# Splitting q and k on 128 partitions with DMA stacking, normalising dilated P on GpSimd, and merging differential P by one ratio, in a hybrid attention trunk

## The chip, the cores and the metric

The kernel runs on one core of a Trainium2 chip. The metric is the device time of one execution in microseconds. A core has five engines, each with its own queue of instructions that it works off in order: TensorE (PE, matrix products; its weight loads are listed as PEld), VectorE (DVE), ScalarE (ACT), GpSimd (POOL) and SyncE (SP), which here issues every DMA. Engines wait for each other by semaphores. TensorE writes to PSUM, the other engines mostly read and write SBUF, which has 128 partitions.

## The reference, cut to what matters

Two layers; each has two attention branches on the same RMS-normalised input of 512 tokens by 1024 features, all in float32.

```python
def dilated_mixture(q, k, v):            # branch A, 16 heads of 64
    outs = [dilated_pattern(q, k, v, w, d) for (w, d) in DILATED_PAIRS]   # softmax per pattern
    wts = d_all * jnp.exp(m_all - jnp.max(m_all, axis=0))                 # weighted by denominators
    return jnp.sum(wts[..., None] * o_all, axis=0) / jnp.sum(wts, axis=0)[..., None]

def one_block(args):                     # branch B, 8 heads with two q/k maps of 64, values of 128
    sc = jnp.einsum('mbqhd,mbkhd->mbhqk', qblk, ks) * (dh ** -0.5)        # causal mask follows
    p = jax.nn.softmax(sc, axis=-1)
    a = p[0] - lam * p[1]
    return jnp.einsum('bhqk,bkhe->bqhe', a, vf)
...
    qa = partial_rope(qa.reshape(b, s, A_HEADS, HEAD_DIM), cos, sin)      # also ka, qb, kb
    ob = rms_norm(ob, subln_w, SUBLN_EPS) * (1.0 - lam_init)
    merged = sigmoid(ga) * (ya @ w_proj_a) + sigmoid(gb) * (yb @ w_proj_b)
    return x + merged @ w_out
```

## The kernel before

Every product that has to be as exact as float32 is made of three float32r products: each operand is split into a part `hi` with fewer bits and the rest, `lo`, and `hi*hi + hi*lo + lo*hi` is summed in PSUM. A split is one ACT pass (the copy that rounds) and one DVE pass (the difference).

Weights come as 207 half chunks of 512 rows by 256 columns, 512 KB each, in the order of use. SP loads them into three buffers `raw` (L75); ACT writes `whi` (L84), DVE `wlo` (L85), and the buffer is free for the next load when DVE is through.

Projections come in two forms: `proj_T` (L164 to L166, tiles `pj`) gives two blocks of 128 features by 512 tokens, in 512-column matmuls; `proj_V` (L216 to L218, tiles `pv`) gives four blocks of 128 tokens by 256 columns. Attention heads are worked in units: a pair of heads in branch A (u = 0 to 7) and a head with its two maps in branch B (u = 0 to 7), 16 units per layer, written (layer, branch, u). While the projections of the next unit run on PE, the scores of the present unit and the values of the one before are spread between their steps (`run`, `mix`, L460 and L675). The order on each engine, and with it the semaphores, comes from a scheduler that simulates the program; it is not written out by hand, so a change of the passes also changes where other instructions stand.

The steps that matter here:

- **q and k** (`ev_qk`, L231): of the projection in PSUM, DVE makes a shuffled copy `sw` (L234) and the product with a cosine table (L236), POOL multiplies `sw` by the sine table (L237), DVE adds (L238). The result `rot` holds two heads (or maps), one on partitions 0 to 63 and one on 64 to 127. S needs q of a head as [hi; lo] stacked on 128 partitions, and k as [lo; hi] and [hi; lo] (tiles `qx`, and `kx` for either half). ACT and DVE write these on 64 partitions at a time: for q L243 to L246, for each half of k L252 to L255.
- **S** (`s_steps`): four blocks of queries per half; L300 and L305/L306 are the matmuls, L307 adds the bias and takes the row minimum (S is negated), L308 makes the exponential and its sum `den`.
- **Normalising** (`norm` in `a_pair`): DVE takes 1/den (L348) and multiplies P's four blocks of 128, 256, 384 and 512 columns by it (L351). In branch B `comb` (L397) scales both maps and adds them, the second with minus lambda (L404, L405).
- **P transposed and values**: L325 transposes P on PE, L326 and L327 split it, L359 and L415 are the products with V. V's own split is L270 and L271. In branch B each output row is then normalised by its root mean square: squares summed by ACT (L427), the inverse root on POOL (L132), four scalings on DVE (L432), and a transposition (`turn`).

Of the kernel before, what the change touches and what calls it, by code (L numbers as in the profile page):

```python
# [9 lines left out]
F32 = mybir.dt.float32  # L10
# [22 lines left out]
def trunk_kernel(ctx: ExitStack, tc: tile.TileContext, x, win, wpa, wpb, wout, norm_w, subln_w, final_w, lams,  # L33
# [24 lines left out]
    # ---------------------------------------------------------------- weights  # L58
    # Half chunks of 512 rows by 256 columns, in the order of use: loaded ahead, then split into
    # a part with float32r's 12 bits and the rest, which float32r holds exactly.  # L60
# [28 lines left out]
    # -------------------------------------------------------------- constants  # L89
# [13 lines left out]
    # P transposed; pt1 keeps a block of zeros  # L103
# [7 lines left out]
    # ------------------------------------------------------ residual and norm  # L111
    def h_block(layer, m, xt):
        """hi and lo parts of x * norm_w; 1/rms comes in after the projections"""
        h = b4(f"h{layer}_{m}")
        nc.scalar.activation(h[:, 0], xt, AF.Copy, scale=nw[:, layer, m:m + 1])  # L115
        nc.vector.scalar_tensor_tensor(h[:, 1], xt, nw[:, layer, m:m + 1], bits(h[:, 0]), OP.mult, OP.subtract)  # L116
        st_["hnew"][m] = h

    def sq_block(m, xt):
        """the running sum of squares, but for the last block's"""  # L120
# [13 lines left out]
    def rstd_cols():  # L134
        """per-token 1/rms as columns [token, token block]"""
# [23 lines left out]
    # ------------------------------------------------------------ projections  # L159
    def mm3(ps, hb, wi, kk, c0, first, last):  # L160
        """ps += w[:, c0:c0+128].T @ h over one block of 128 rows, in three passes"""
# [8 lines left out]
    def proj_T(rhs, evac, first=False):  # L170
        """Two output blocks, features on partitions. rhs(k) gives the moving block."""
# [27 lines left out]
    def proj_V(lhs, evac):  # L199
        """256 columns, tokens on partitions. lhs(k) gives the stationary block."""  # L200
# [29 lines left out]

    def ev_qk(key):  # L231
        def f(b, ps):
# [6 lines left out]
            lo, hi = slice(0, 64), slice(64, 128)  # L239
            if b == 0:  # L240
                qx = b4(f"qx{key}")
                # S' = -scale * q.k: the sign makes the row maximum a minimum
                nc.scalar.activation(qx[lo, 0], r[lo], AF.Copy, scale=-SCALE)  # L243
                nc.scalar.activation(qx[hi, 1], r[hi], AF.Copy, scale=-SCALE)
                nc.vector.scalar_tensor_tensor(qx[hi, 0], r[lo], -SCALE, bits(qx[lo, 0]), OP.mult, OP.subtract)
                nc.vector.scalar_tensor_tensor(qx[lo, 1], r[hi], -SCALE, bits(qx[hi, 1]), OP.mult, OP.subtract)  # L246
                st_["qk"][key] = [qx]
            else:
                # against a head's [hi; lo] of q: [lo; hi] of k, and [hi; lo] of k
                for half, (mine, other) in enumerate(((lo, hi), (hi, lo))):  # L250
                    kx = b4(f"kx{key}{half}")
                    nc.scalar.activation(kx[mine, 1], r[mine], AF.Copy)  # L252
                    nc.vector.tensor_tensor(kx[mine, 0], r[mine], bits(kx[mine, 1]), OP.subtract)
                    nc.scalar.activation(kx[other, 0], bits(kx[mine, 1]), AF.Copy)
                    nc.vector.tensor_copy(kx[other, 1], bits(kx[mine, 0]))  # L255
# [3 lines left out]
    def ev_v(key, br):  # L259
        def f(tb, ps):  # L260
# [4 lines left out]
            # per head: the columns' hi parts, then their lo parts  # L265
# [18 lines left out]
    # -------------------------------------------------------------- attention  # L284
    def s_steps(key, half, br, store):
# [6 lines left out]
        def s(i):  # L292
# [5 lines left out]
            if i == 0:  # L298
                # 256 columns hold both products, which float32r's full rate needs
# [33 lines left out]
    def pt_block(j, i, s):  # L333
        """P transposed: keys of block j, queries of block i"""
# [5 lines left out]
    def a_pair(layer, u):  # L340
        """two heads of the dilated mixture"""
# [4 lines left out]
        def norm(half):  # L346
            r = small.tile([P, 4], F32, tag="r", name=f"r{key}{half}")
            nc.vector.reciprocal(r, store["den", half])  # L348
            for i in range(4):
                p = store["p", half][i]  # L350
                nc.vector.tensor_scalar(p, p, r[:, i:i + 1], None, OP.mult)  # L351
# [39 lines left out]
    def b_head(layer, u):  # L391
        """one head of the differential attention"""
# [402 lines left out]
```

## Time and profile before

| | |
|---|---|
| median of 3 runs | 1399.28 us (1399.16, 1399.28, 1399.30) |
| span of the profiled execution | 1397.3 us |
| PE busy | 1380.0 us (99%) |
| DVE busy | 1047.4 us (75%) |
| ACT busy | 795.7 us (57%) |
| POOL busy | 152.5 us (11%) |
| DMA, mean over the span | 94 GB/s |

The span is that of the instructions in the profiled execution; the time of a run also holds what lies around it, some 2 us. An engine's busy time counts the time in which it executes, not that in which it waits. The profile names an instruction by engine, line and tile, and where an engine stood idle before it, the length of that and what released it. "s(0, 0, 3)10" is block 0 of half 1 of the unit (0, 0, 3).

### The profile page before, as it was taken

The page shows a single profiled execution, that of the slowest core. Times are in us where ns is not written, and L with a number is a line of the kernel's source. Part 1 is how long each engine was busy: PE and PEld are TensorE (multiplying, and loading weights), DVE is VectorE, ACT ScalarE, POOL GpSimd, SP SyncE. Part 2 cuts the span into 40 slices and gives each one's busy share as a digit, 9 for nine tenths or more (in the row PEclk, how much of TensorE's full clock was granted, in tenths as well). Part 3 has the DMA queues.
Part 4 walks back from the last instruction along what each step waited for, and adds up shares of the span by engine and source line. Part 5 has one row for each costly group of instructions (what it writes and reads, how often), then busy time and mean ns, then how long its engine had stood idle before and what let it go on. Part 6 is the DMA issues. An engine that isn't in the chain of part 4 may idle for free.

```text
span 1397.3 us, 20366 instructions
## 1 busy us (share of the span) xinstructions
PE 1380.0 (99%) x7592; PEld 1192.9 (85%) x7592; DVE 1047.4 (75%) x2188; ACT 795.7 (57%) x1530; POOL 152.5 (11%) x123
## 2 busy tenths in 40 slices
PE   7999999999999999999999999999999999999998
PEld 6888898989888888888888888988888988888898
DVE  6899989985678886445558989999865889763554
ACT  4666666665456666333445767666645666653333
POOL 3201000100101111110211000110000111111000
PEclk9999999999999999999999999999999999999999
DMA  6222212223331233332532212122233222333421
GB/s 215 97 61 76 76 61 86 66 76 106 113 98 62 73 109 121 106 106 91 188 99 82 70 61 91 61 76 76 83 114 106 76 76 76 98 113 120 152 90 62
DMA packets 41954, 131.66 MB, mean 94 GB/s; under 512 B 4864, under 2 KB 4992, under 8 KB 41856
## 3 DMA queue, kind: packets, MB, share of 16 engines
q1 hardware_dynamic: 41856, 130.38, 28.8%
q8 instruction: 59, 0.97, 0.3%
q14 instruction: 39, 0.32, 0.1%
HBM read 121.97 MB, written 8.39 MB: 93 GB/s over the span
## 4 chain that ended last, share of the span: by engine, by line
PE 86%; DVE 10%; issue 2%; ACT 1%; DMA 0%; POOL 0%; SPq 0%; POOLq 0%; DVEq 0%; ACTq 0%
PE pj L164 20%; PE pj L165 20%; PE pj L166 20%; PE pv L216 4%; PE pv L218 4%; PE pv L217 4%; DVE wlo L85 2%; DVE pt L327 1%; DMA x<-x_d 0%; DVE h L116 0%; PE xt L553 0%; PE ps_ss L140 0%; ACT whi L84 0%; ACT h L115 0%; POOL rf L570 0%
## 5 line engine op out<-in xcount | busy, mean ns | idle before, releaser
L164 PE MATMUL pj<-h,whi 128*128 128x512 f32 x1024 | 409.8, 402 | 6.3 <-DVE whi L610 6.0
L165 PE MATMUL pj<-h,whi 128*128 128x512 f32 x1024 | 404.8, 396 | 1.0 <-DVE h L116 0.9
L166 PE MATMUL pj<-h,wlo 128*128 128x512 f32 x1024 | 403.7, 396 | 0.1
L85 DVE TENSOR_TENSOR wlo<-raw,whi 128x1024 fp32r<-128x1024 f32 x207 | 273.0, 1320 | 85.4 <-ACT whi L84 84.6
L84 ACT ACTIVATE whi<-raw 128x1024 fp32r<-128x1024 f32 x207 | 218.3, 1055 | 148.9 <-PE pj L165 104.3
L164 PEld LDWEIGHTS pj<-h,whi 128*128 128x128 f32 x1024 | 193.4, 189 | 41.8 <-issue 6.0
L166 PEld LDWEIGHTS pj<-h,wlo 128*128 128x128 f32 x1024 | 193.0, 188 | 40.1 <-DVE wlo L85 0.5
L165 PEld LDWEIGHTS pj<-h,whi 128*128 128x128 f32 x1024 | 193.4, 189 | 35.8 <-DVE h L116 2.7
L216 PE MATMUL pv<-whi,h 128*128 128x256 f32 x512 | 146.7, 287 | 2.2 <-DVE v(0, 0, 0)_0_399 L271 1.6
L217 PE MATMUL pv<-wlo,h 128*128 128x256 f32 x512 | 144.9, 283 | 0.0
L218 PE MATMUL pv<-whi,h 128*128 128x256 f32 x512 | 144.8, 283 | 0.0
L216 PEld LDWEIGHTS pv<-whi,h 128*128 128x128 f32 x512 | 97.5, 190 | 4.5 <-DVE v(0, 0, 0)_0_399 L271 1.8
L217 PEld LDWEIGHTS pv<-wlo,h 128*128 128x128 f32 x512 | 97.6, 191 | 0.9
L218 PEld LDWEIGHTS pv<-whi,h 128*128 128x128 f32 x512 | 97.5, 191 | 0.0
L506 POOL TENSOR_TENSOR g<-g,pr 128x512 f32<-128x512 f32 x16 | 21.7, 1354 | 162.4 <-ACT g L505 162.4
L503 DVE TENSOR_TENSOR g<-pj,rb 128x512 f32<-128x512 f32 x32 | 21.8, 688 | 23.4 <-PE pj L166 23.3
L217 PE MATMUL pv<-wlo,mg 128*128 128x256 f32 x128 | 35.8, 283 | 0.0
L218 PE MATMUL pv<-whi,mg 128*128 128x256 f32 x128 | 35.7, 283 | 0.0
L216 PE MATMUL pv<-whi,mg 128*128 128x256 f32 x128 | 35.4, 283 | 0.0
L514 DVE TENSOR_TENSOR g<-pj,g 128x512 f32<-128x512 f32 x16 | 11.1, 692 | 30.5 <-PE pj L166 30.5
L126 POOL TENSOR_TENSOR sq<-sq,sq 128x512 f32<-128x512 f32 x12 | 19.2, 1598 | 85.8 <-ACT sq L122 85.5
L518 ACT ACTIVATE mg<-g 128x512 fp32r<-128x512 f32 x16 | 10.1, 631 | 29.5 <-DVE g L515 29.5
(4991 smaller groups left out, 2903.8 us busy)
## 6 DMA issues: line engine op xcount, KB each, us to landing
raw<-win_d SPq DMA_DIRECT2D x159, 512.0 KB, 3.5
raw<-wpa_d SPq DMA_DIRECT2D x16, 512.0 KB, 3.5
raw<-wpb_d SPq DMA_DIRECT2D x16, 512.0 KB, 3.5
raw<-wout_d SPq DMA_DIRECT2D x16, 512.0 KB, 3.5
pa_dram<-pa SPq DMA_DIRECT2D x16, 256.0 KB, 2.0
pr<-pa_dram SPq DMA_DIRECT2D x16, 256.0 KB, 3.9
xr<-x_d SPq DMA_DIRECT2D x8, 256.0 KB, 4.1
x_dram<-xr SPq DMA_DIRECT2D x8, 256.0 KB, 2.6
```

The costliest lines, as they stand in the source:

```text
L84: nc.scalar.activation(whi[j], raw[j], AF.Copy)
L85: nc.vector.tensor_tensor(wlo[j], raw.pop(j), bits(whi[j]), OP.subtract)
L126: nc.gpsimd.tensor_tensor(st_["acc"], st_["acc"], s, OP.add)
L164: nc.tensor.matmul(ps, w_h, hb[:, 0], start=first, stop=False)
L165: nc.tensor.matmul(ps, w_h, hb[:, 1], start=False, stop=False)
L166: nc.tensor.matmul(ps, w_l, hb[:, 0], start=False, stop=last)
L216: nc.tensor.matmul(ps, hh, whi[wi][:, k % 4], start=(k == 0), stop=False)
L217: nc.tensor.matmul(ps, hh, wlo[wi][:, k % 4], start=False, stop=False)
L218: nc.tensor.matmul(ps, hl, whi[wi][:, k % 4], start=False, stop=(k == 7))
L327: nc.vector.tensor_tensor(dst[:, 1], ps[:, :n], bits(dst[:, 0]), OP.subtract)
L503: nc.vector.tensor_tensor(g[:, b], ps, rb, OP.mult)
L506: nc.gpsimd.tensor_tensor(g[:, 0], g[:, 0], st_.pop(("pa", m)), OP.mult)
```

## The change

`ev_qk` makes the hi and the lo part of q, and of k, in one pass each on all 128 partitions, into a new tile `hl` (from the same pool of 27 buffers). SP then copies 64-partition pieces by DMA into `qx` (four moves of 128 KB) and `kx` (per half one move of 256 KB and two of 128 KB). In branch A the four multiplications of P by 1/den go from DVE to POOL. In branch B P is merged as p1 + q*p2 with q = -lambda*den1/den2, without the scaling of p1 by r = 1/den1, which is applied with the output: in the squares (as `scale`) and in one pass that multiplies the output by r times the inverse root.

```diff
+    def move(to, of):
+        nc.sync.dma_start(bits(to), bits(of))
 ...
-            lo, hi = slice(0, 64), slice(64, 128)
+            hl = b4(f"hl{key}{b}")
+            f_ = -SCALE if b == 0 else 1.0
+            nc.scalar.activation(hl[:, 1], r, AF.Copy, scale=f_)
+            nc.vector.scalar_tensor_tensor(hl[:, 0], r, f_, bits(hl[:, 1]), OP.mult, OP.subtract)
             if b == 0:
                 qx = b4(f"qx{key}")
-                nc.scalar.activation(qx[lo, 0], r[lo], AF.Copy, scale=-SCALE)
-                nc.scalar.activation(qx[hi, 1], r[hi], AF.Copy, scale=-SCALE)
-                nc.vector.scalar_tensor_tensor(qx[hi, 0], r[lo], -SCALE, bits(qx[lo, 0]), OP.mult, OP.subtract)
-                nc.vector.scalar_tensor_tensor(qx[lo, 1], r[hi], -SCALE, bits(qx[hi, 1]), OP.mult, OP.subtract)
+                for half in range(2):
+                    mine = slice(64 * half, 64 * half + 64)
+                    move(qx[0:64, half], hl[mine, 1])
+                    move(qx[64:128, half], hl[mine, 0])
                 st_["qk"][key] = [qx]
             else:
-                for half, (mine, other) in enumerate(((lo, hi), (hi, lo))):
+                for half in range(2):
                     kx = b4(f"kx{key}{half}")
-                    nc.scalar.activation(kx[mine, 1], r[mine], AF.Copy)
-                    nc.vector.tensor_tensor(kx[mine, 0], r[mine], bits(kx[mine, 1]), OP.subtract)
-                    nc.scalar.activation(kx[other, 0], bits(kx[mine, 1]), AF.Copy)
-                    nc.vector.tensor_copy(kx[other, 1], bits(kx[mine, 0]))
+                    mine = slice(64 * half, 64 * half + 64)
+                    move(kx[0:64], hl[mine])
+                    move(kx[64:128, 0], hl[mine, 1])
+                    move(kx[64:128, 1], hl[mine, 0])
 ...
-                nc.vector.tensor_scalar(p, p, r[:, i:i + 1], None, OP.mult)
+                nc.gpsimd.tensor_scalar(p, p, r[:, i:i + 1], None, OP.mult)
 ...
-            r = [small.tile([P, 4], F32, tag=f"rb{h}", name=f"rb{key}{h}") for h in range(2)]
-            for h in range(2):
-                nc.vector.reciprocal(r[h], store["den", h])
-            nc.vector.tensor_scalar(r[1], r[1], nlam[:, layer:layer + 1], None, OP.mult)
+            r = small.tile([P, 4], F32, tag="rb0", name=f"rb{key}")
+            q = small.tile([P, 4], F32, tag="rb1", name=f"rq{key}")
+            nc.vector.reciprocal(q, store["den", 1])
+            nc.vector.reciprocal(r, store["den", 0])
+            nc.vector.scalar_tensor_tensor(q, q, nlam[:, layer:layer + 1], store["den", 0], OP.mult, OP.mult)
+            store["r"] = r
             for i in range(4):
                 p, p2 = store["p", 0][i], store["p", 1][i]
-                nc.vector.tensor_scalar(p, p, r[0][:, i:i + 1], None, OP.mult)
-                nc.vector.scalar_tensor_tensor(p, p2, r[1][:, i:i + 1], p, OP.mult, OP.add)
+                nc.vector.scalar_tensor_tensor(p, p2, q[:, i:i + 1], p, OP.mult, OP.add)
 ...
+                r = store["r"][:, i:i + 1]
-                nc.scalar.activation(scr, o[:, n], AF.Square, accum_out=store["ss"][:, i:i + 1])
+                nc.scalar.activation(scr, o[:, n], AF.Square, scale=r, accum_out=store["ss"][:, i:i + 1])
 ...
-                for i in range(4):
-                    nc.vector.tensor_scalar(store["o"][:, i], store["o"][:, i], r[:, i:i + 1], None, OP.mult)
+                nc.vector.tensor_tensor(r, r, store["r"], OP.mult)
+                o = store["o"]
+                nc.vector.tensor_tensor(o, o, r.unsqueeze(2).to_broadcast([P, 4, P]), OP.mult)
```

The scheduler puts instructions in another order. On PE, at the first unit of layer 0, the kernel before has the end of the fourth block of V's projection (`pv_3`), six matmuls of the next q projection (`pj_0`), and then the first S:

```order
L216 MATMUL pv_3_457<-whi_334,h_7_172 128x256
L217 MATMUL pv_3_457<-wlo_335,h_7_172 128x256
L218 MATMUL pv_3_457<-whi_334,h_7_172 128x256
L164 MATMUL pj_0_515<-h_0_123,whi_368 128x512
L165 MATMUL pj_0_515<-h_0_123,whi_368 128x512
L166 MATMUL pj_0_515<-h_0_123,wlo_369 128x512
L164 MATMUL pj_0_515<-h_1_128,whi_368 128x512
L165 MATMUL pj_0_515<-h_1_128,whi_368 128x512
L166 MATMUL pj_0_515<-h_1_128,wlo_369 128x512
L300 MATMUL s(0, 0, 0)00_522<-kx(0, 0, 0)0_358,qx(0, 0, 0)_316 128x256
```

The changed kernel has there, on the same engine, at the end of the third block (`pv_2`):

```order
L216 MATMUL pv_2_433<-whi_337,h_7_172 128x256
L217 MATMUL pv_2_433<-wlo_338,h_7_172 128x256
L218 MATMUL pv_2_433<-whi_337,h_7_172 128x256
L307 MATMUL s(0, 0, 0)00_526<-kx(0, 0, 0)0_364,qx(0, 0, 0)_319 128x256
L312 MATMUL s(0, 0, 0)01_538<-kx(0, 0, 0)0_364,qx(0, 0, 0)_319 128x256
L313 MATMUL s(0, 0, 0)01_538<-kx(0, 0, 0)0_364,qx(0, 0, 0)_319 128x256
L216 MATMUL pv_3_461<-whi_279,h_0_123 128x256
```

S of the first two blocks of queries has moved ahead of the whole fourth block, 24 matmuls, and of the six of the q projection. It is the same in layer 1.

On SP, at units (0,0,6) and (0,0,7), the queue of the kernel before holds weight loads alone:

```order
L75 DMA raw_2224<-win_d 128x1024
L75 DMA raw_2264<-win_d 128x1024
L75 DMA raw_2351<-win_d 128x1024
L75 DMA raw_2415<-win_d 128x1024
L75 DMA raw_2498<-win_d 128x1024
L75 DMA raw_2550<-win_d 128x1024
```

In the changed kernel the moves of a unit stand between them (x2 is two alike in a row):

```order
L75 DMA raw_2292<-win_d 128x1024
L232 DMA qx(0, 0, 7)_2347<-hl(0, 0, 7)0_2344 64x512 x2
L75 DMA raw_2382<-win_d 128x1024
L232 DMA qx(0, 0, 7)_2347<-hl(0, 0, 7)0_2344 64x512 x2
L75 DMA raw_2447<-win_d 128x1024
L232 DMA kx(0, 0, 7)0_2422<-hl(0, 0, 7)1_2419 64x512
L232 DMA kx(0, 0, 7)0_2422<-hl(0, 0, 7)1_2419 64x1024
L232 DMA kx(0, 0, 7)0_2422<-hl(0, 0, 7)1_2419 64x512
L232 DMA kx(0, 0, 7)1_2426<-hl(0, 0, 7)1_2419 64x1024
L232 DMA kx(0, 0, 7)1_2426<-hl(0, 0, 7)1_2419 64x512 x2
L75 DMA raw_2530<-win_d 128x1024
```

Ten moves per unit now stand in the one queue with the weights.

## Rows read from the trace of the kernel before

**Rows 1.** The page's first part: busy time, share of the span and number of instructions of each engine.

```profile
PE 1380.0 (99%) x7592; PEld 1192.9 (85%) x7592; DVE 1047.4 (75%) x2188; ACT 795.7 (57%) x1530; POOL 152.5 (11%) x123
```

**Rows 2.** The waits of PE, the whole answer: who waited for whom, total us, times, longest us.

```profile
PE pj L164 <- DVE whi L610: 6.0, 1, 6.0
PE pv L216 <- DVE v(0, 0, 0)_0_399 L271: 1.6, 1, 1.6
PE pj L165 <- DVE h L116: 0.9, 1, 0.9
PE s(1, 0, 3)10_7983 L300 <- DVE mn(1, 0, 3)0_7812 L307: 0.7, 1, 0.7
PE s(0, 0, 3)10_1457 L300 <- DVE mn(0, 0, 3)0_1286 L307: 0.5, 1, 0.5
PE pv L216 <- DVE v(1, 0, 1)_0_7383 L271: 0.3, 1, 0.3
PE pv L216 <- DVE v(0, 0, 1)_0_857 L271: 0.3, 1, 0.3
PE pj L164 <- DVE v(1, 1, 3)_1_11531 L271: 0.2, 1, 0.2
PE pj L164 <- DVE v(0, 1, 3)_1_5005 L271: 0.2, 1, 0.2
```

**Rows 3.** Timeline of PE, 42 to 56 us: start, length (pipelined, so longer than the distance to the next), engine, line, output and inputs; in brackets idle time before it and its releaser.

```profile
42.99 0.28 PE L218 MATMUL pv<-whi,h 128*128 128x256 f32 x1
44.90 0.39 PE L216 MATMUL pv<-whi,h 128*128 128x256 f32 x1 [1.63 <-DVE v(0, 0, 0)_0_399 L271]
...
47.88 0.40 PE L164 MATMUL pj<-h,whi 128*128 128x512 f32 x1
...
49.27 0.28 PE L300 MATMUL s(0, 0, 0)00_522<-kx(0, 0, 0)0_358,qx(0, 0, 0)_316 128*128 128x256 f32 x1
...
53.29 0.39 PE L164 MATMUL pj<-h,whi 128*128 128x512 f32 x1
...
55.33 0.39 PE L165 MATMUL pj<-h,whi 128*128 128x512 f32 x1
```

**Rows 4.** Timeline of ACT and of DVE at the first unit of layer 0, columns as above.

```profile
40.34 0.63 ACT L243 ACTIVATE qx(0, 0, 0)_316<-rot(0, 0, 0)0_312 64x512 fp32r<-64x512 f32 x1 [2.46 <-DVE rot(0, 0, 0)0_312 L238]
...
41.23 0.69 DVE L245 SCALAR_TENSOR_TENSOR qx(0, 0, 0)_316<-rot(0, 0, 0)0_312,qx(0, 0, 0)_316 64x512 fp32r<-64x512 f32 x1
...
42.21 0.69 DVE L246 SCALAR_TENSOR_TENSOR qx(0, 0, 0)_316<-rot(0, 0, 0)0_312,qx(0, 0, 0)_316 64x512 fp32r<-64x512 f32 x1
...
44.37 0.48 DVE L271 SCALAR_TENSOR_TENSOR v(0, 0, 0)_0_399<-pv,rstd,v(0, 0, 0)_0_399 128x256 fp32r<-128x256 f32 x1
```

**Rows 5.** The page's part on DMA issues (count, KB each, median us from issue to landing), and two issues in a row from SP's timeline at the start.

```profile
raw<-win_d SPq DMA_DIRECT2D x159, 512.0 KB, 3.5
...
pa_dram<-pa SPq DMA_DIRECT2D x16, 256.0 KB, 2.0
...
1.65 0.42 SPq L596 DMA_DIRECT2D raw<-win_d  x1
2.12 0.43 SPq L595 DMA_DIRECT2D x<-x_d  x1
```

**Rows 6.** Timelines of DVE, ACT and PE at the first unit of layer 1.

```profile
723.80 1.68 DVE L238 TENSOR_TENSOR rot(1, 0, 0)0_6853<-rot(1, 0, 0)0_6853,sw(1, 0, 0)0_6851 128x512 f32<-128x512 f32 x1
...
725.51 0.63 ACT L243 ACTIVATE qx(1, 0, 0)_6857<-rot(1, 0, 0)0_6853 64x512 fp32r<-64x512 f32 x1 [1.52 <-DVE rot(1, 0, 0)0_6853 L238]
...
727.96 0.69 DVE L246 SCALAR_TENSOR_TENSOR qx(1, 0, 0)_6857<-rot(1, 0, 0)0_6853,qx(1, 0, 0)_6857 64x512 fp32r<-64x512 f32 x1
...
735.25 0.28 PE L300 MATMUL s(1, 0, 0)00_7048<-kx(1, 0, 0)0_6899,qx(1, 0, 0)_6857 128*128 128x256 f32 x1
```

**Rows 7.** Timelines of DVE, ACT and PE: k of unit (0,0,4) from its add to its first S, and the reciprocal and the first transpose of unit (0,0,3), half 0.

```profile
141.29 0.69 DVE L238 TENSOR_TENSOR rot(0, 0, 4)1_1414<-rot(0, 0, 4)1_1414,sw(0, 0, 4)1_1412 128x512 f32<-128x512 f32 x1
...
142.73 0.62 ACT L252 ACTIVATE kx(0, 0, 4)0_1418<-rot(0, 0, 4)1_1414 64x512 fp32r<-64x512 f32 x1
...
143.09 0.16 DVE L348 RECIPROCAL r(0, 0, 3)0_1400<-den(0, 0, 3)0_1287 128x4 f32<-128x4 f32 x1
...
146.68 0.42 DVE L255 CAST kx(0, 0, 4)0_1418<-kx(0, 0, 4)0_1418 64x512 fp32r<-64x512 f32 x1
...
152.69 0.28 PE L300 MATMUL s(0, 0, 4)00_1645<-kx(0, 0, 4)0_1418,qx(0, 0, 4)_1346 128*128 128x256 f32 x1
...
154.20 0.27 PE L325 MATMUL t((0, 0, 3), 0)0_1657<-ident,p(0, 0, 3)00_1304 128*128 128x128 f32 x1
```

**Rows 8.** The waits of SP's DMA queue, first row: total us, times, longest us.

```profile
SPq L75 <- DVE wlo L85: 719.2, 125, 13.8
```

**Rows 9.** Instructions of the lines L237 and L351: count, then shortest, median and longest ns, and start.

```profile
L237 POOL TENSOR_TENSOR sw(0, 0, 0)0_310<-sw(0, 0, 0)0_310,st x1: 1305/1305/1305, 36.1 to 36.1; 128x512 f32<-128x512 f32 x1
L237 POOL TENSOR_TENSOR sw(0, 0, 0)1_352<-sw(0, 0, 0)1_352,st x1: 2279/2279/2279, 37.3 to 37.3; 128x512 f32<-128x512 f32 x1
...
L351 DVE TENSOR_SCALAR p(0, 0, 0)00_523<-p(0, 0, 0)00_523,r(0, 0, 0)0_575 x1: 288/288/288, 59.9 to 59.9; 128x128 f32<-128x128 f32 x1
...
L351 DVE TENSOR_SCALAR p(0, 0, 0)03_570<-p(0, 0, 0)03_570,r(0, 0, 0)0_575 x1: 480/480/480, 60.7 to 60.7; 128x512 f32<-128x512 f32 x1
```

**Rows 10.** Busy time by stretches, from 9 to 13 us: length, then busy us and instructions of PE, PEld, DVE, ACT and POOL; granted clock, DMA's busy share, GB/s.

```profile
9.00:13.00 4.00, 4.00 (x18) 3.18 (x18) 2.98 (x5) 4.00 (x7) 0.67 (x1) 1.00 1.04 400
```

## The prediction

> **What bounds the kernel now.** I read the busy shares first: PE is busy 1380.0 of 1397.3 us, DVE 1047.4, ACT 795.7, POOL 152.5 [rows 1]. With an engine at 99%, work taken off the others is worth only the time for which PE waits for them, so the second view is the list of PE's waits, and it is the whole budget: 6.0 us and 0.9 us at the start (the first weights and the first h), 1.6 us before the fourth block of the first V projection, and six of 0.7 down to 0.2 us, 2.2 us together [rows 2]. The change touches neither the start nor the tail. It can win at most 1.6 + 2.2 = 3.8 us of waits, 0.27%; whatever it makes PE wait anew is lost in full. So the question is where PE is close behind its inputs, and this is at the first head of each layer.
>
> The granted clock is 1.00 throughout. PE's own pace: from 47.88 to 49.27 us six 512-column matmuls start in 1.39 us, 0.232 each; from 53.29 to 55.33, when DVE stands idle, nine start in 2.04 us, 0.227 each [rows 3]. I come back to that 2% as a rival.
>
> **The change part by part, q and k.** Before, a head's split costs ACT 6 and DVE 6 passes on 64 partitions, and S waits for the last of kx. Now ACT and DVE make one 128-partition pass each per block (4 in all) and SP issues ten SBUF-to-SBUF moves per head, four for qx and three for each kx, 1.5 MB. A pass on 128 partitions costs what one on 64 does (0.69 us for DVE's q pass on 64 [rows 4] and for its rope add on 128 [rows 7]), so 8 passes per head go. That frees time on engines which do not bound; what counts is when the first kx is there. Two moving parts: the issue on SP, 0.47 us from one to the next when they stand back to back [rows 5], and the flight. No row shows a transfer from SBUF to SBUF. The nearest are the 256 KB store of A's projection, 2.0 us from issue to landing, and the 512 KB weight load, 3.5 us [rows 5]; moves of 128 and 256 KB lie nearer the first. I bound the last landing by these two, and take 2.7.
>
> *First head of layer 0.* ACT begins q's hi at 40.34 and, in one pass, ends at 40.97. DVE's q pass starts at 41.23 and k's takes the place of the second q pass, at 42.21, and ends near 42.9 [rows 4]. SP issues q's moves from 41.0 on, k's first three at 42.95, 43.42 and 43.9. So kx for S0 lands between 45.9 and 47.4. Meanwhile the order on PE changes: S0 stands right behind block 2 of the V projection, where it stood behind block 3 and six more matmuls. PE is through block 2 at 43.27 (the last matmul starts at 42.99 and takes 0.28), and before, it then lost 1.63 us to the v evacuation, going on at 44.90 [rows 3]. That wait goes, as DVE comes to the evacuation (44.37 before [rows 4]) without the two kx passes ahead of it; but S0's wait stands in the same place and ends later. Net loss: 45.9 - 44.9 = 1.0 to 47.4 - 44.9 = 2.5; I take +1.7. The score reductions on DVE and the exponentials on ACT now stand ahead of the next weight split, which moves with S0; by an estimate from these passes' lengths it is still ready about 1 us before PE needs it, so it adds nothing.
>
> *First head of layer 1.* The same order on PE. S0 started at 735.25 [rows 6]; without block 3 (24 matmuls at 0.12 us, 2.88) and six at 0.232 (1.39) ahead of it, it is due at 730.98. ACT's q pass ends at 726.14 and DVE's k pass takes the place of the second q pass, ending near 728.65 [rows 6]. Three issues: 728.7, 729.2, 729.65; landing 731.65 to 733.15. Loss 0.7 to 2.2, I take +1.5. There was no wait here before to set against it.
>
> *The other 30 heads.* In the order, 17 to 22 us of PE work lie between the end of a k projection and its S0 for A heads (13.5 us for the second head of a layer), and more for B. In head (0,0,4) the k chain runs from DVE's add at 141.29, behind the product on POOL, to the last copy of the first kx, 146.68 + 0.42 = 147.1; S0 comes at 152.69 [rows 7]. Now: add ends 141.98, ACT's hi, behind what is queued there, again at 142.73 and until 143.4, lo until 144.1, three issues 1.4, flight 2.0 to 3.5: 147.5 to 149.0. That leaves 3.7 us. I cost these heads at nothing; the cover is those 3.7 us, and beyond it each us counts per head. Each DMA of SP's queue also waits for the one eight places earlier in the queue; in a burst of ten this reaches back to the head's own q moves, issued some 2 us or more earlier, so only kx's second half can feel it.
>
> SP's queue carries the weights as well. 320 issues at 0.33 to 0.47 us are about 130 us of SP's time, and moves that wait for DVE hold the next weight load behind them. But the loads now wait 719 us in 125 cases, up to 13.8 us, for a buffer to come free [rows 8], and a load is used several projections later: a delay of a few us is covered. Zero.
>
> **Normalising on GpSimd.** DVE loses per half four passes of 0.29 to 0.48 us, 1.5 together [rows 9], and POOL gets them. No row shows this pass on POOL. Bounds: 1.5 us if it goes at DVE's speed, 5.2 if each costs the 1.30 of POOL's 128x512 product, 9.0 if each costs the 2.28 that this product took beside DVE work [rows 9]. I take 4, nearer the undisturbed product. Its readers are the transposes: in head (0,0,3) the reciprocal comes at 143.09 and the first transpose at 154.20, 11 us later [rows 7]; over all halves of the new order the stretch from the last S matmul to the first transpose is at least 12 us of PE work, of which reduction, exponential and reciprocal take some 4. Hidden up to about 8 us. Behind it on POOL stands the next head's rope product, and behind that DVE's add, which blocks DVE's queue: this too is covered at 4 us. The two engines slow each other (DVE's add took 0.69 in head (0,0,4) and 1.68 beside POOL at the start of layer 1 [rows 6, 7]), at worst 1 us per collision on a chain that has 3.7. Zero, with the far bound kept for a rival.
>
> [...]
>
> **The merge in B.** Per head four TENSOR_SCALARs (the shapes of [rows 9], 1.5 us) and four of 0.28 become one pass over the output. PE has no wait on this chain in [rows 2]. Gain 0. Some 250 more semaphore waits on PE's queue run ahead of execution: 0.
>
> **The later waits.** The six of 2.2 us hang on DVE being late by less than 1 us (the reduction of S, v's evacuation) [rows 2]. DVE has 1.5 us less per half and eight passes less per head ahead of them. I count all 2.2 as won.
>
> **Sum.** +1.7 + 1.5 - 2.2 = +1.0 us. The profiled execution spans 1397.3; the median of 1399.28 has 2.0 us around the span, and the three runs lie within 0.01%, so the same 2.0 is added: 1397.3 + 1.0 + 2.0 = **1400.3**. Bounds by the two landings: 1.0 + 0.7 - 2.2 = -0.5 to 2.5 + 2.2 - 2.2 = +2.5, 1398.8 to 1401.8.
>
> **Rivals.**
> *Moves at half rate.* The moves go from 64 partitions to 64, and may use half of what a 128-partition load gets. The fastest stretch moved 400 GB/s [rows 10]; at 200, the 1 MB of q and of the first kx's bytes lasts 5.2 us from 41.0, and with the 1.4 to 2.0 us of a store's flight that is not bytes, it lands at 47.6 to 48.2: +3.0. In layer 1 a weight load lies between: 733.3 to 733.9, +2.6. Sum 3.0 + 2.6 - 2.2 = +3.4, 1402.7, just slower. For it: the shape; against it: the issue at 0.47 us per 128 KB is nearly as slow.
>
> [...]
>
> *POOL or SP blocks head by head* (ends slower). Place: the rope product behind the normalising on POOL, DVE's add behind it. Decides when a half costs POOL over about 8 us, or a move's flight exceeds 7. Price: 1 us beyond the cover in each of some 26 heads, +26: 1426. For it: 2.28 us in [rows 9]; against: the same product takes 1.30 where DVE is not in its way [rows 9].
>
> *The later waits don't go,* since DVE's order there is new too: +1.7 + 1.5 + 0 = +3.2, 1402.5.
>
> *PE's pace.* If the 2% between the two stretches of [rows 3] came from what the engines beside it do, and half of DVE's relief gave it back in the two A parts of some 215 us each: 430 x 1% = -4.3, sum -3.3, 1396.0, faster. For it: DVE is idle in one stretch and not in the other; against it: nothing in [rows 2] names an engine for it.
>
> **How the numbers follow.** Forecast 0.50 (1400.3; within 0.2%). Half rate 0.20 (three quarters slower, one quarter within). Head by head 0.10 (slower). Later waits stay 0.10 (half slower). Pace 0.10 (faster). Measurement of this kernel can tell about 0.2%, 2.8 us, from no change. Faster 0.10; slower 0.15 + 0.10 + 0.05 = 0.30, and with the upper tail of the forecast 0.33; same 0.57. The range 1396.0 to 1404.5 takes in all but the head-by-head case and the ends.
>
> **What would show it.** PE's list of waits: a wait of S(0,0,0)0 on SPq of 2.6 to 4.1 us in place of 1.6 on L271, one of 0.7 to 2.2 for S(1,0,0)0, and no entries of L307 or L271. The moves' landing in the DMA part: 2.0 to 3.5. The normalising rows on POOL: under 8 us a half. I am wrong if PE waits for other heads' kx or for transposes, or if its 512-column pace changes.

## The result: 0.72% slower, and the profile after

The changed kernel takes 1409.46 us (median of 4 runs, 1407.22 to 1411.30) against 1399.22 for the kernel before; the ratio is 1.0072, 95% interval 1.0057 to 1.0086. The forecast was 1400.3 with a range of 1396.0 to 1404.5. The profiled execution spans 1409.5 us, 12.2 more than the one of before.

First the busy shares of the changed kernel, which answer to [rows 1]:

```profile
PE 1384.4 (98%) x7592; PEld 1197.9 (85%) x7592; DVE 914.5 (65%) x1836; ACT 718.2 (51%) x1402; POOL 317.9 (23%) x251
```

DVE lost 133 us of work and ACT 78, and none of it came out at the end. PE's waits in the changed kernel say why; they answer to [rows 2] (total us, times, longest us):

```profile
PE pj L164 <- DVE whi L621: 5.9, 1, 5.9
PE s(1, 0, 0)00_7068 L307 <- DMA kx(1, 0, 0)0_6921<-hl(1, 0, 0)1_6918: 5.6, 1, 5.6
PE s(0, 0, 0)00_526 L307 <- DMA kx(0, 0, 0)0_364<-hl(0, 0, 0)1_361: 5.1, 1, 5.1
PE pj L165 <- DVE h L116: 1.1, 1, 1.1
PE s(1, 0, 1)00_7225 L307 <- DMA kx(1, 0, 1)1_7204<-hl(1, 0, 1)1_7197: 0.9, 1, 0.9
```

The 1.6 us on v's evacuation and the six small waits are gone. In their place S of the first unit waits for its moves, 5.1 us in layer 0 and 5.6 in layer 1, and the second unit of layer 1 waits 0.9.

That is not all. PE's timeline around the wait in layer 0 (answers to [rows 3]):

```profile
43.19 0.28 PE L217 MATMUL pv<-wlo,h 128*128 128x256 f32 x1
43.31 0.28 PE L218 MATMUL pv<-whi,h 128*128 128x256 f32 x1
48.64 0.55 PE L307 MATMUL s(0, 0, 0)00_526<-kx(0, 0, 0)0_364,qx(0, 0, 0)_319 128*128 128x256 f32 x1 [5.05 <-DMA kx(0, 0, 0)0_364<-hl(0, 0, 0)1_361]
...
49.42 0.41 PE L216 MATMUL pv<-whi,h 128*128 128x256 f32 x1
49.63 0.41 PE L217 MATMUL pv<-wlo,h 128*128 128x256 f32 x1
...
54.36 0.40 PE L164 MATMUL pj<-h,whi 128*128 128x512 f32 x1
```

Behind the wait, 256-column matmuls start every 0.21 us where they started every 0.12 ahead of it. The stretches of the same kernel tell what changed (length; busy us and instructions of PE, PEld, DVE, ACT, POOL; granted clock, DMA's busy share, GB/s):

```profile
40.00:43.00 3.00, 3.00 (x27) 3.00 (x27) 2.86 (x12) 2.21 (x3) 0.00 (x0) 1.00 0.57 193
43.00:49.00 6.00, 0.95 (x7) 0.78 (x7) 1.63 (x7) 1.63 (x5) 0.00 (x0) 0.86 0.94 214
49.00:50.00 1.00, 1.00 (x6) 1.00 (x6) 0.64 (x2) 0.00 (x0) 0.00 (x0) 0.50 0.76 186
...
53.00:54.00 1.00, 1.00 (x7) 1.00 (x6) 0.65 (x1) 0.32 (x1) 0.00 (x0) 0.50 0.00 0
54.00:55.00 1.00, 1.00 (x7) 0.91 (x7) 0.58 (x1) 0.44 (x2) 0.00 (x0) 0.94 0.00 0
55.00:56.00 1.00, 1.00 (x6) 0.81 (x6) 0.48 (x1) 0.98 (x2) 0.00 (x0) 1.00 0.63 66
```

PE stood idle for 5.05 us, the granted clock fell from 1.00 to 0.50, and it stayed there until about 54.1. The 27 matmuls from 48.64 to 54.36 took 5.72 us; at 0.12 each they take 3.24. So the wait cost another 2.5 us after it was over. In layer 1 the 27 from 741.08 to 746.98 took 5.90, 2.7 too many:

```profile
741.08 0.55 PE L307 MATMUL s(1, 0, 0)00_7068<-kx(1, 0, 0)0_6921,qx(1, 0, 0)_6876 128*128 128x256 f32 x1 [5.56 <-DMA kx(1, 0, 0)0_6921<-hl(1, 0, 0)1_6918]
...
746.98 0.42 PE L164 MATMUL pj<-h,whi 128*128 128x512 f32 x1
```

The account of the 12.2 us: 5.1 - 1.6 in layer 0, 5.6 in layer 1, 0.9 in its second unit, 2.5 + 2.7 for the low clock: +15.2. The remaining 3.0 us, by difference, are what the rest of the change gives back.

Where the lateness comes from: SP's issues of the first unit of layer 0 and of k in layer 1 (start, length of the group), and the moves' times from issue to landing in 40 to 50 us, then in 728 to 744 (KB each, median us):

```profile
41.31 2.44 SPq L232 DMA_DIRECT2D qx(0, 0, 0)_319<-hl(0, 0, 0)0_316  x4
43.85 1.88 SPq L232 DMA_DIRECT2D kx(0, 0, 0)0_364<-hl(0, 0, 0)1_361  x3
...
733.58 2.71 SPq L232 DMA_DIRECT2D kx(1, 0, 0)0_6921<-hl(1, 0, 0)1_6918  x3
```

```profile
kx(0, 0, 0)0_364<-hl(0, 0, 0)1_361 SPq DMA_DIRECT2D x2, 128.0 KB, 3.2
...
raw<-win_d SPq DMA_DIRECT2D x1, 512.0 KB, 5.8
kx(1, 0, 0)0_6921<-hl(1, 0, 0)1_6918 SPq DMA_DIRECT2D x1, 256.0 KB, 6.4
kx(1, 0, 0)0_6921<-hl(1, 0, 0)1_6918 SPq DMA_DIRECT2D x2, 128.0 KB, 6.2
```

An issue takes 0.6 us, not 0.47, so k's first goes out at 43.85 instead of 42.95 (0.3 us of this is that everything before it runs 0.3 later). And the moves run at 214 GB/s with the DMA engines 94% busy (the row 43 to 49), where loads ran at 400 [rows 10]. In layer 1 a weight load shares the burst, k's three issues take 2.71 us, and the first kx needs over 6 us from issue to landing.

POOL took somewhat more than the prediction gave it (line L358: shortest, median, longest ns): 4.3 us in the first half, shown here, against the 4 taken. Over all 32 halves it is some 5.2 us, since POOL's busy time grew by 165.4 us (152.5 to 317.9) for these 128 passes. PE never waits for it.

```profile
L358 POOL TENSOR_SCALAR p(0, 0, 0)00_527<-p(0, 0, 0)00_527,r(0, 0, 0)0_582 x1: 611/611/611, 60.0 to 60.0; 128x128 f32<-128x128 f32 x1
L358 POOL TENSOR_SCALAR p(0, 0, 0)01_539<-p(0, 0, 0)01_539,r(0, 0, 0)0_582 x1: 924/924/924, 60.6 to 60.6; 128x256 f32<-128x256 f32 x1
L358 POOL TENSOR_SCALAR p(0, 0, 0)02_551<-p(0, 0, 0)02_551,r(0, 0, 0)0_582 x1: 1244/1244/1244, 61.5 to 61.5; 128x384 f32<-128x384 f32 x1
L358 POOL TENSOR_SCALAR p(0, 0, 0)03_577<-p(0, 0, 0)03_577,r(0, 0, 0)0_582 x1: 1568/1568/1568, 62.7 to 62.7; 128x512 f32<-128x512 f32 x1
```

### The profile page after: what moved, and what is told of

Read it like the earlier page. It is cut to its first block, busy times and chain, and to the rows that moved or that the text cites. A ratio compares the mean times of both kernels' runs of the same rounds, so it can differ in the third digit from the quotient of the medians.

```text
span 1409.5 us, 21036 instructions
## 1 busy us (share of the span) xinstructions
PE 1384.4 (98%) x7592; PEld 1197.9 (85%) x7592; DVE 914.5 (65%) x1836; ACT 718.2 (51%) x1402; POOL 317.9 (23%) x251
## 4 chain that ended last, share of the span: by engine, by line
PE 95%; DVE 2%; DMA 1%; issue 1%; ACT 1%; SPq 0%; POOL 0%; POOLq 0%; ACTq 0%
PE pj L164 22%; PE pj L165 21%; PE pj L166 21%; PE pv L216 5%; PE pv L218 5%; PE pv L217 5%; DMA x<-x_d 0%; DMA kx(1, 0, 0)0_6921<-hl(1, 0, 0)1_6918 0%; DVE h L116 0%; DVE wlo L85 0%; DMA kx(1, 0, 1)1_7204<-hl(1, 0, 1)1_7197 0%; PE xt L564 0%; PE ps_ss L140 0%; DMA kx(0, 0, 0)0_364<-hl(0, 0, 0)1_361 0%; SPq L232 0%
## 5 line engine op out<-in xcount | busy, mean ns | idle before, releaser
L85 DVE TENSOR_TENSOR wlo<-raw,whi 128x1024 fp32r<-128x1024 f32 x207 | 276.0, 1334 | 111.7 <-ACT whi L84 108.5
L216 PE MATMUL pv<-whi,h 128*128 128x256 f32 x512 | 148.5, 290 | 0.0
L218 PE MATMUL pv<-whi,h 128*128 128x256 f32 x512 | 146.5, 286 | 0.0
L216 PEld LDWEIGHTS pv<-whi,h 128*128 128x128 f32 x512 | 99.4, 194 | 1.0
L218 PEld LDWEIGHTS pv<-whi,h 128*128 128x128 f32 x512 | 99.3, 194 | 0.1
```

The source lines that it names most:

```text
L85: nc.vector.tensor_tensor(wlo[j], raw.pop(j), bits(whi[j]), OP.subtract)
L216: nc.tensor.matmul(ps, hh, whi[wi][:, k % 4], start=(k == 0), stop=False)
L218: nc.tensor.matmul(ps, hl, whi[wi][:, k % 4], start=False, stop=(k == 7))
```

## The experiments

My theory after the result: the loss is the exposed moves at the two layer starts plus the low clock behind them, and everything else in the change is harmless or a small gain. The rivals: POOL costs it; the moves cost a little in every unit; the slow matmuls have another cause than PE's idleness.

### Which part of the change

**Only the split and its moves** (normalising back on DVE, branch B's merge as before):

```diff
-                nc.gpsimd.tensor_scalar(p, p, r[:, i:i + 1], None, OP.mult)
+                nc.vector.tensor_scalar(p, p, r[:, i:i + 1], None, OP.mult)
...
+                nc.vector.tensor_scalar(p, p, r[0][:, i:i + 1], None, OP.mult)
+                nc.vector.scalar_tensor_tensor(p, p2, r[1][:, i:i + 1], p, OP.mult, OP.add)
...
```

> The changed kernel with the normalising of branch A back on DVE and branch B's merge as before; only the 128-partition split and its DMA moves are left of the change. Theory A (the loss is PE's wait for the first kx of either layer, 5.1 and 5.6 us, and the halved clock that follows it, about 2.5 us each): as slow as the changed kernel, 1406 to 1412 us, with the same two waits in PE's list and a granted clock of 0.50 behind them. Rival B (the normalising on POOL costs the time): back near 1399.

Measured 1406.79 us, ratio 1.0051 (1.0036 to 1.0067). S0 waits 4.9 and 4.7 us. POOL (rival B) falls: without its work three quarters of the loss stay, 7.6 of 10.2 us.

The parts do not add up, though. The changed kernel is 2.7 us slower than the split alone (1409.46 against 1406.79; all its runs lie above all runs of this one, though the two intervals overlap). In the traces the difference is in layer 1: S0 waits 5.6 us instead of 4.7, the 27 matmuls behind it take 5.90 instead of 4.78, and the second unit's 0.9 us are not there. Whether POOL's work or the merge causes this is not shown.

**All but the moves** (`ev_qk` as before, normalising on POOL and the merge kept):

```diff
-            hl = b4(f"hl{key}{b}")
...
+                nc.vector.scalar_tensor_tensor(qx[hi, 0], r[lo], -SCALE, bits(qx[lo, 0]), OP.mult, OP.subtract)
```

> The changed kernel with q and k made on 64 partitions as before, no moves; normalising on POOL and the merge are kept. Theory A: 1396 to 1399 us, no wait of S on a DMA, clock 1.00. Rival B (POOL): 1404 or more.

Measured 1394.77 us, ratio 0.9968 (0.9955 to 0.9980): 4.4 us faster than before, more than the range expected. Of the 4.4 us between the two profiled spans, 2.9 are idle time of PE (17.3 to 14.4) and 1.5 its busy time (1380.0 to 1378.5) for the same 7592 matmuls; why these took less is open. PE's list holds two rows:

```profile
PE pj L164 <- DVE whi L617: 6.2, 1, 6.2
PE pv L216 <- DVE v(0, 0, 0)_0_399 L274: 1.6, 1, 1.6
```

**The normalising alone, and the merge alone,** each on the kernel before:

```diff
-                nc.vector.tensor_scalar(p, p, r[:, i:i + 1], None, OP.mult)
+                nc.gpsimd.tensor_scalar(p, p, r[:, i:i + 1], None, OP.mult)
```

> The kernel before with the normalising of branch A on POOL, nothing else changed. Theory F1 (the 4.4 us that the changed kernel without moves gains come from DVE being ahead in branch A, where PE had its small waits): 1394 to 1396.5 us, no wait of S on L307 in PE's list. Rival F2 (they come from the merge in branch B, or from both): 1397 to 1399.3.

```diff
-                nc.vector.tensor_scalar(p, p, r[0][:, i:i + 1], None, OP.mult)
-                nc.vector.scalar_tensor_tensor(p, p2, r[1][:, i:i + 1], p, OP.mult, OP.add)
+                nc.vector.scalar_tensor_tensor(p, p2, q[:, i:i + 1], p, OP.mult, OP.add)
...
```

> The kernel before with branch B's merge by one ratio, nothing else changed. If the gain of the changed kernel without moves is the sum of its two parts (norm alone gave 2.7 of 4.4 us): 1397 to 1398.2. If the merge gives nothing on its own, as the prediction had it: 1398.7 to 1399.7.

The normalising alone gives 1396.63 us, ratio 0.9982 (0.9973 to 0.9991), just outside F1's range, with no wait of S on the reduction. The merge alone gives 1398.83, ratio 0.9996 (0.9987 to 1.0005): no difference, as the prediction had it. Of the six small waits of [rows 2] the four in branch A go with the normalising, and the two of 0.2 us at v(0, 1, 3) and v(1, 1, 3) with the merge. That both together come out 1.9 us under the normalising alone is not settled, since the intervals 0.9955 to 0.9980 and 0.9973 to 0.9991 overlap.

### Is it the layer starts alone

**The first unit of each layer by ACT and DVE, 30 units by moves:**

```diff
-        return lambda: proj_T(hrhs, ev_qk((layer, br, u)))
+        return lambda: proj_T(hrhs, (ev_qk_compute if (br, u) == (0, 0) else ev_qk)((layer, br, u)))
```

> The changed kernel, but the first unit of each layer makes qx and kx on ACT and DVE as before; the other 30 units keep their moves. Theory A: 1397 to 1400 us, of PE's waits on DMA at most the 0.9 us of the second unit of layer 1 is left. Rival C (320 moves on SP's queue cost a little in every unit, through weight loads or DVE): 1404 or more.

Measured 1395.94 us, ratio 0.9976 (0.9967 to 0.9985), no wait on any DMA. The time lies 1.1 us under the range expected. Two units of 32 hold the whole loss, and rival C falls. The other 30 units' moves bring nothing either: the interval overlaps with that of the kernel without moves, and if anything they cost some 1.2 us, as all ten runs (from 1395.28 up) lie above all five of that kernel (up to 1395.18).

**All moves, but S0 where it was:**

```diff
-            run(chain(*[todo[n[0]](layer, *n[1:]) for n in names]), side)
+            with tc.manual_schedule(engines={mybir.EngineType.PE}) if w == 0 else nullcontext():
+                run(chain(*[todo[n[0]](layer, *n[1:]) for n in names]), side)
```

> The changed kernel with all its moves, but PE keeps the order in which the program is written through the first unit's window of each layer, so that S of the first unit stands behind the fourth V block and some projection matmuls again, as in the kernel before. Theory A1 (it is the place of S0 that exposes the moves, they land at about 48.3 us): S0 comes up at about 48.7, waits under 1 us, clock 1.00, 1397 to 1401 us. Rival A2 (the moves are late wherever S0 stands): waits of 2 us or more in both layers, 1404 or more.

Measured 1397.85 us, ratio 0.9992 (0.9983 to 1.0000). The first stretch and the waits of PE:

```profile
43.00:49.00 6.00, 5.13 (x34) 4.79 (x35) 3.67 (x11) 3.51 (x6) 0.00 (x0) 1.00 0.93 217
```

```profile
PE s(1, 0, 0)00_7073 L307 <- DMA kx(1, 0, 0)1_6928<-hl(1, 0, 0)1_6921: 1.1, 1, 1.1
PE pv L216 <- DVE v(0, 0, 0)_0_403 L278: 0.9, 1, 0.9
```

The moves are as slow as in the changed kernel, 217 GB/s at a share of 0.93, but PE works off V's last block meanwhile: S0 of layer 0 comes up without a wait and the clock stays at 1.00. A1 holds for layer 0; in layer 1 a wait of 1.1 us is left, just over its bound. The moves' slowness becomes a loss through the place that the scheduler gave S0.

### Is the low clock idleness

Both kernels write S0 out behind block 2, as the scheduler had placed it; one puts 40 matmuls that nobody reads into the gap of each layer.

```diff
+        steps = chain(qk(layer, 0, 0), vv(layer, 0, 0))
+        with tc.manual_schedule(engines={mybir.EngineType.PE}):
+            run(steps[:-8])
+            early = heads[0][0](0)
...
+            for _ in range(FILL):
+                nc.tensor.matmul(fill[:, :256], h0[:, 0, :P], h0[:, 0, :256], start=True, stop=True)
+            early[0][1]()
+            early[1][1]()
+            run(steps[-8:])
```

> The changed kernel with S's first two blocks of the first unit written out behind block 2 of the V projection, the place which the scheduler gave them in the changed kernel; the control for the next run. Both theories: as the changed kernel, 1406 to 1412 us, S0 waits 4.7 to 5.6 us in either layer, and where PE's clock is 0.50 behind the wait, 27 matmuls take 5.7 us instead of 3.2.

> As the control, with 40 matmuls of 256 columns, whose results nobody reads, between block 2 and S0 in each layer: 80 matmuls more, 9.6 us of PE work, put where PE stood idle. Theory A (the low clock comes from PE's idleness, some 2.5 us each time it falls): clock 1.00 throughout, S0 starts where it did or up to 0.5 us later, and the kernel is 2 to 5 us faster than the control although it computes more: 1402 to 1406. Rival D (the slow matmuls behind the wait come from something else at that place, the moves' traffic or the semaphores): the slow pace stays, 1406 to 1412 as the control.

Control 1409.12 us, ratio 1.0071 (1.0059 to 1.0084); with the filling 1406.66, ratio 1.0054 (1.0040 to 1.0068). Two stretches of layer 1, of the control, then of the filled kernel:

```profile
735.00:741.00 6.00, 1.89 (x9) 1.92 (x10) 1.27 (x6) 1.52 (x2) 0.00 (x0) 0.75 0.76 168
741.00:747.00 6.00, 6.00 (x30) 5.63 (x30) 2.15 (x3) 3.06 (x7) 0.00 (x0) 0.69 0.16 35
```

```profile
735.00:741.00 6.00, 5.52 (x47) 5.34 (x46) 1.00 (x3) 1.61 (x2) 0.00 (x0) 1.00 0.93 192
741.00:747.00 6.00, 6.00 (x39) 5.41 (x38) 3.69 (x9) 3.69 (x8) 0.00 (x0) 1.00 0.25 76
```

With 80 matmuls more the kernel is 2.5 us faster (0.7 above the range expected): the clock stays at 1.00 at both places, and the 6 us from 741 hold 39 matmuls instead of 30. The 27 matmuls from S0 on take 3.30 us in either layer, where the control takes 4.80 and 5.80. All runs of the filled kernel lie under all runs of the control, though the two intervals overlap a little. So the low pace is PE's idleness (rival D falls). The expectation on S0 failed in layer 0: with the filling it starts at 50.05 instead of 48.32, as its moves of 128 KB land in 4.6 instead of 3.2 us there; why is open. The control's two clock drops cost 1.5 and 2.5 us, 4.0 and not 5; in layer 0 the later landing took nearly all of the 1.5 back, so most of the gain is layer 1's.

### Issue or bytes

**k's moves on ACT's queue:**

```diff
-    def move(to, of):
-        nc.sync.dma_start(bits(to), bits(of))
+    def move(to, of, eng=None):
+        (eng or nc.sync).dma_start(bits(to), bits(of))
...
+                    move(kx[0:64], hl[mine], nc.scalar)
...
```

> The changed kernel with k's six moves of every unit issued by ACT's queue, q's four left on SP's. Theory E1 (the first kx is late because seven issues of 0.6 us stand one behind another on SP): k's first issue goes out near 42.9 instead of 43.85 us, the first kx lands near 47.3 instead of 48.3, S0's waits are about 1 us shorter in each layer, 1404 to 1409 us. Theory E2 (the bytes bound, 214 GB/s with every DMA engine 94% busy in 43 to 49 us): the landing stays within 0.4 us of 48.3 and the time within 2 us of the changed kernel's. Either could lose a few us elsewhere, since ACT spends 0.6 us per issue.

The time, 1431.86 us (ratio 1.0233, 1.0219 to 1.0247), is in neither range. In layer 0 it answers the question:

```profile
42.21 2.10 ACTq L232 DMA_DIRECT2D kx(0, 0, 0)0_364<-hl(0, 0, 0)1_361  x3
44.35 3.00 ACTq L232 DMA_DIRECT2D kx(0, 0, 0)1_368<-hl(0, 0, 0)1_361  x3
47.45 0.84 ACT L277 ACTIVATE v(0, 0, 0)_0_403<-pv,rstd 128x256 fp32r<-128x256 f32 x2 [5.27 <-DMA kx(0, 0, 0)0_364<-hl(0, 0, 0)1_361]
```

k's issue goes out 1.6 us earlier, but its moves then take 3.7 to 4.0 us to land instead of 3.0 to 3.2, and S0 starts at 48.35, only 0.3 earlier. That is E2's answer: the bytes bind. The new loss is another: ACT itself stands behind its own moves, here for 5.27 us and in two dozen other units for 3.6 to 7.0, and PE's list gets 15 further waits, up to 3.1 us. This is the prediction's head-by-head rival, in a queue that it had not named.

**Moves on all 128 partitions.** The same bytes, as ten moves with 1 KB rows or six with 2 KB rows; S multiplies other numbers then. Shown is the edit for six; for ten, q's moves are cut in two by columns, and each kx goes as its first 256 columns in one move of 256 KB and the others in two of 128 KB.

```diff
-                    move(qx[0:64, half], hl[mine, 1])
-                    move(qx[64:128, half], hl[mine, 0])
+                    move(qx[:, half], hl[:, half])
...
-                    move(kx[0:64], hl[mine])
-                    move(kx[64:128, 0], hl[mine, 1])
-                    move(kx[64:128, 1], hl[mine, 0])
+                    move(kx[:, 0], hl[:, 0])
+                    move(kx[:, 1], hl[:, 1])
```

> The changed kernel with every move from 128 to 128 partitions instead of 64 to 64, ten per unit with the same bytes as before; q and k are then not stacked as S needs them, so S multiplies other numbers. Rows are 1 KB long instead of 2 KB. Theory G1 (the moves are slow because they reach 64 partitions, 214 GB/s at 94% busy engines): in 43 to 48 us the rate rises to 300 GB/s or more, the first kx lands under 2.7 us after its last issue, S0 waits at most 4 us in layer 0 and at most 4.5 in layer 1. Rival G2 (copies from SBUF to SBUF are slow in any shape): rate within 10% of 214, S0 waits as before, 5.1 and 5.6 us.

> As the run before, with six moves of 256 KB per unit in place of ten, so that rows are 2 KB long again. The scheduler puts S0 of layer 0 behind V's last block here, so it is the landing that tells, not the sum. G1: 256 KB lands 2.0 to 2.6 us after its issue, as the store of A's projection does, and the rate in the burst is 300 GB/s or more. G2: 3 us or more, 214 GB/s.

Ten moves: 1402.80 us, ratio 1.0025 (1.0015 to 1.0035), S0 waits 3.6 and 2.4 us. Six: 1395.13, ratio 0.9970 (0.9958 to 0.9982), no wait on a DMA; here the scheduler also put S0 later in layer 0, so the sum is not the moves' alone. The stretches tell the rate, first of the changed kernel, then of the one with six:

```profile
43.00:45.00 2.00, 0.58 (x5) 0.38 (x4) 1.42 (x7) 1.63 (x5) 0.00 (x0) 1.00 0.90 207
45.00:47.00 2.00, 0.00 (x0) 0.00 (x0) 0.21 (x1) 0.00 (x0) 0.00 (x0) 1.00 0.94 196
```

```profile
43.00:45.00 2.00, 1.10 (x9) 0.89 (x8) 1.28 (x8) 1.82 (x5) 0.00 (x0) 1.00 0.97 364
45.00:47.00 2.00, 2.00 (x19) 2.00 (x18) 0.41 (x2) 0.54 (x1) 0.00 (x0) 1.00 0.96 365
```

Then of the one with ten:

```profile
43.00:45.00 2.00, 0.00 (x0) 0.00 (x0) 1.19 (x3) 0.77 (x3) 0.00 (x0) 1.00 0.57 197
45.00:47.00 2.00, 0.43 (x2) 0.46 (x3) 0.00 (x0) 0.00 (x0) 0.00 (x0) 0.92 0.81 277
```

At nearly the same busy share six 128-partition moves carry 365 GB/s and ten 64-partition ones 200; 256 KB lands in 2.3 to 2.6 us, within G1's 2.0 to 2.6. With ten 128-partition moves, the 300 GB/s of G1 are not reached, since the engines are busy for only 0.57 and 0.81 of the time: issuing limits instead (in layer 0 the ten issues take SP 6.4 us, 0.64 each), and S0 still waits. Yet for each share of busy time the ten carry as much as the six (277 at 0.81, 365 at 0.96) and far more than the 64-partition moves (196 at 0.94), so the rate goes with the partitions and not with the number of moves. So both were short: the rate, 196 and 207 GB/s against 365, and behind that seven issues of 0.6 us.

The run with ten also tells something of the clock. In layer 1 S0 waits only 2.4 us, and still the 27 matmuls behind the wait take 4.80 us instead of 3.30:

```profile
PE s(1, 0, 0)00_7068 L305 <- DMA kx(1, 0, 0)0_6921<-hl(1, 0, 0)1_6918: 2.4, 1, 2.4
```

```profile
737.00:738.00 1.00, 1.00 (x7) 1.00 (x6) 0.00 (x0) 0.81 (x3) 0.00 (x0) 0.50 0.00 0
```

S0 starts at 734.91 and the next matmuls at full pace, 0.12 us apart; from 736.2 to 739.6 they start every 0.21 us, at a granted clock of 0.50. So the clock can fall after the wait is over.

### Looking for a faster version

**Without moves, and the lambdas later:**

```diff
-        if layer == 0:
-            lambdas()
...
+            if layer == 0 and w == 4:
+                lambdas()
```

> The changed kernel without its moves (q and k made on 64 partitions as before), and with the lambdas of branch B computed after the fifth window instead of ahead of the first: four reductions on DVE and a table load on ACT leave the stretch from 38 to 46 us where DVE works off q, k and v. Theory: the last wait that is not the start, 1.6 us for the evacuation of v, shrinks to under 0.5, and the time goes from 1394.8 to between 1393 and 1394.5, the fastest so far. Rival: the wait only moves to another input of the same place, 1394.5 to 1395.2.

Measured 1395.09 us, ratio 0.9969 (0.9958 to 0.9981), the same as without this edit and in the rival's range; the wait for v's evacuation fell only from 1.6 to 1.0 us. The fastest kernel stays the one without moves, 1394.77.

## Why the prediction was wrong

**The view was right, and so was the place.** PE's waits were the budget, S0 of the first unit of each layer the exposed instruction, and the six small waits went. The normalising (4 us taken; 4.3 in the first half, 5.2 in the mean, hidden as it was to be), the merge on its own (0) and all but one of the other 30 units (0.9 us) came out as costed. By profiled spans the sum was 11.2 us short (+1.0 against +12.2): 1.8 in layer 0, 4.1 in layer 1, 0.9 in the second unit, 5.2 for the clock, less 0.8 more given back than the 2.2 taken.

The first half's four passes, 4.3 us on POOL, took DVE 1.5 before (0.29 to 0.48 each [rows 9]); hidden as they are, this changed nothing.

What two of the zeros rested on, the traces show. In the one of before, the ninth to the fifteenth DMA of SP's queue each wait for the one eight places earlier: the fifteenth (`sw_in`) goes out at 10.21 us, after a wait of 1.0 us, as the seventh (`raw`) lands at 10.20. On PE's queue the changed kernel has 256 semaphore instructions of their own, where the kernel before has 111; the longest lasts 3.29 us, from 75.97 on, and PE is busy for all of that time.

**The step that failed is the landing of the first kx, issues and flight, in "First head of layer 0" and "of layer 1".** I bounded the flight by a 128-partition store and a 128-partition load, and gave the case of half the rate 0.20. It was the case (196 to 217 GB/s, against 365 on 128 partitions). In layer 0 the net loss was 5.1 - 1.6 = 3.5 us against 1.7 (range 1.0 to 2.5). About half of the difference is the issues, 0.6 us each instead of 0.47, and half the flight: S0 started 3.6 us after the last of the three issues (45.07), where I took 2.7. Issued faster, the bytes would have held it up nearly as long, as the run with k on ACT's queue shows. The rival had the landing at 47.6 to 48.2, and S0 started at 48.64. In layer 1 the loss was 5.6 against 1.5, and most of that is the flight: 6.2 us from the last of the three issues (734.83) to S0. The weight load in the burst slowed down as well (5.8 us instead of 3.5). The rival had only 2.6 there, and was low by its own terms: worked as in layer 0, 726.1 + 5.2 + 1.4 to 2.0 is 732.7 to 733.3 without the weight load, so that its 733.3 to 733.9 left 0.6 us for 512 KB, which take 2.6 at 200 GB/s.

**A term was missing altogether: PE's clock behind a wait.** Each of the two waits was followed by 5.5 and 5.9 us at 0.50, which cost 2.5 and 2.7 us more, a third of the 15.2 us lost. It is the largest error of the sum; without it, by this account, the kernel would have come out near 1404.3, at the upper end of the range. In the trace of before no wait behind the start was longer than 1.6 us, and that one left the clock at 1.00. But the start itself had a sign of it. Behind the wait of 6.0 us for the first weights, the first seven matmuls of 512 columns take 3.02 us, 0.43 each, where the 18 of the next stretch take 0.22 each [rows 10]:

```profile
5.00:9.00 4.00, 3.02 (x7) 2.47 (x8) 3.07 (x6) 0.80 (x2) 0.00 (x0) 1.00 0.96 332
```

The profile's clock column reads 1.00 there, so this row does not name the clock; but the pace is the half one of the 0.50 stretches (0.21 for 256 columns), and the prediction passed over it. The half-rate rival with this term gives 1402.7 + 5.2 = 1407.9, within the four runs, but partly by luck: its layer 1 was 3.0 us too short.

**The gain was too small.** 2.2 us for the later waits; the two parts without moves gave 4.4, of which 1.5 lie in PE's busy time and not in any wait. The normalising alone gave 2.7. The rival "PE's pace" had the direction of those 1.5 us, with 4.3; its cause is not shown.

**What the scheduler did** I read right and priced too low. That it put S0 behind block 2 because its model has kx ready there is likely, but no run shows the model's times. With the moves as they are, S0 in its old place waits for nothing in layer 0 and 1.1 us in layer 1.

**Open:** why the low clock lasts differently from run to run (the 27 matmuls take 4.78 us after a wait of 4.7 us in the run with the split alone, 5.80 after 4.8 in the control of the filling, both in layer 1); why layer 1 loses more with the whole change than with the split alone; why the filled kernel's moves landed later in layer 0; and whether the merge adds something beside the normalising.

## What to carry to other kernels

With one engine at 99%, look at the few places where its inputs arrive just in time, and price a new transfer by rows of its own shape: partitions, count of issues, and what shares its burst. A wait on PE can cost more than itself: here the granted clock fell to 0.50 with waits of 2.4 to 5.6 us, and the two waits of the changed kernel, 5.1 and 5.6 us, cost 2.5 and 2.7 more in that way. Look for the pace behind any long wait, the one at the start too. Putting the waiting instruction later, so that useful work fills the gap, gave back 11.6 us here (1397.85 against 1409.46); ten moves on 128 partitions, with the instruction left where it was, gave back 6.7 (1402.80). If a scheduler moves the consumer of a new transfer up, check that place first.

## What the runs showed of the hardware that was not expected

- The granted clock fell to 0.50 with PE's waits of 5.05 and 5.56 us, and in the run with ten 128-partition moves with waits of 3.6 and 2.4 us, the last 1.3 us after PE was at work again; it stood at 1.00 after waits of 0.9, 1.1 and 1.6 us. Filling the gap with unread matmuls made the kernel 2.5 us faster.
- Moves between SBUF tiles of 64 partitions: 196 to 217 GB/s with the DMA engines 90 to 94% busy; of 128 partitions: 365.
- A one-input multiplication on POOL takes 1.57 us for 128x512, where DVE takes 0.48 [rows 9].
- An SBUF-to-SBUF issue takes 0.6 us of SP in a burst; on ACT's queue it also holds ACT behind its own moves, 5.27 us at the first unit.
